# Adding DMAs and one tile at a time at the ends of an encoder's steps

## The chip, the core and the metric

The kernel runs on one core of a Trainium2 chip. The metric is the device time of one execution in microseconds. The core has five engines with an instruction stream each: TensorE (PE in the profile; its weight loads are PEld), VectorE (DVE), ScalarE (ACT), GpSimd (POOL) and SyncE (SP). Each engine works through its own stream in order, and streams wait for each other only through semaphores. DMAs are issued here from SyncE's stream, and those that add to what stands in the target from GpSimd's.

## What is computed

The reference is a trunk of two layers over 512 tokens of width 1024, in float32:

```
layer 0:  x += 0.5*ffn(norm(x));  x += mixer_s5_gla(norm(x));     x += 0.5*ffn(norm(x))
layer 1:  x += 0.5*ffn(norm(x));  x += mixer_retention(norm(x));  x += 0.5*ffn(norm(x))
out = norm(x)

norm(x) = x * rsqrt(mean(x*x) + 1e-6) * g
ffn(h)  = (silu(gate) * up) @ w2,   gate, up = split(h @ w1)      # hidden width 2816
```

The first mixer is a diagonal state space model (S5) beside a gated linear attention (GLA), with one projection in and one out. The second is a retention with eight heads. Each is run in both directions.

## The kernel before

All of x stays on the chip as eight tiles x[0] to x[7] of 128x512 (128 of the 1024 channels, by 512 tokens). Float32 products are made on TensorE as three products of rounded parts: mm3 (L196 to L198) multiplies high by high, high by low and low by high. So every operand is needed as a high and a low part. A weight unit (128x1024, 512 KB) is loaded by SyncE into `raw` (4 buffers), ScalarE casts it to `wh`, and `wl` = raw - wh is made in one of two ways (`weights`): by a subtraction on VectorE (L185, called plain), or by ScalarE writing -raw cast to `wl` (L191) and GpSimd issuing a DMA that adds raw to it (L192). Both `wh` and `wl` have 3 buffers.

The program has six steps, and this text calls their ends A to F: the first ffn (end A), the S5 and GLA mixer (end B), two ffns in a row by a scheme with seven products in place of eight blocks (`ffn7`; ends C and D), the retention mixer (end E), and a third ffn7 that finishes the output (end F). A step's last part makes the tiles of x one after the other. As soon as x[n] is there, `prep(n, ...)` makes the operands of the next step: `operand` one high and one low tile (L105, L106), and `operand7` the blocks that ffn7 needs. For tiles 0 to 3 these are b and n (L118 to L123). For tiles 4 to 7 they are ta, b2h, b2l, n23h, n23l and n4 (L130 to L139). Then `squares` (L158, L159) squares x[n] on ScalarE into a tile `sq` and adds it on GpSimd to `sumsq`.

The tiles sq, the difference of halves in `operand7` and its n4 all come from the pool with the tag `tb`, which has two buffers. The norm's factor is not applied to the operands. The next step begins with matmuls on the operands as they are, and somewhat later in TensorE's order stands a matmul of ones with `sumsq` (L166, `rstd`), from which the factor of each token comes. That matmul needs all eight squares. The instructions of each engine are put in order ahead of time, so the matmul's place is fixed.

The outputs of the mixers are matmuls with weight units of two tiles each (12 matmuls a tile and part). The first mixer's output has two parts, part 0 from GLA and part 1 from S5, which are summed in one bank of PSUM. The retention's output has four groups g of heads; each group's products are added to x by VectorE on their own (L1191).

Of the kernel before, what the change touches and what calls it, by code (L numbers as in the profile page):

```python
# [20 lines left out]
ALU = mybir.AluOpType  # L21
# [15 lines left out]
CHUNKS = ((0, 6), (6, 14), (14, 22))  # L37
# [13 lines left out]
def encoder(tc, I, out, dbg=None):  # L51
# [5 lines left out]
    with ExitStack() as ctx:  # L57
# [9 lines left out]
        x = [xs[:, i] for i in range(KT)]  # L67
# [30 lines left out]
        def bank(name="mm"):  # L98
            return pp.tile([128, S], F32, name=name, tag="mm")
# [50 lines left out]
                operand(i, n)  # L150
            squares(i, acc)

        def squares(i, acc):
            if i == 0:
                A.activation(acc, x[i], AF.Square)
            else:
                sq = tmp("tb")
                A.activation(sq, x[i], AF.Square)  # L158
                G.tensor_tensor(acc, acc, sq, op=ALU.add)  # L159

        def new_acc():
            return tp.tile([128, S], F32, name="sumsq", tag="sumsq", bufs=1)
# [114 lines left out]
        def ffn7(w1, w2, acc, nxt, pools, finish=None):  # L277
# [147 lines left out]
            for q, (ks0, ks1) in enumerate(CHUNKS):  # L425
                w2q = w2[0] if q == 0 else w2[1][q - 1]
                for j in range(ks0, ks1):
                    first, last = j == ks0, j == ks1 - 1
                    if j == 0:

                        three, rest = range(3), range(3, 4)
                        p1(0)
                        p1(1)
                        p2(0, three)
                        r2(0, three)
                    elif j != 1:
                        p1(j)
                    ready_22(j)
                    if j + 2 < ks1:
                        load(j + 2)  # L440
                    if not first:
                        r1(j - 1)
                        r3(j - 1)
                    if not last and j > 0:
                        ready_a1(j + 1)
                    ready_13(j)
                    if j == 0:
                        p2(0, rest)
                        r2(0, rest)
                    else:  # L450
                        p2(j)
                        if not last:
                            sums12(j + 1)
                        r2(j)
                        if j == 1:
                            rs = rstd(acc)
                    if not last:
                        if j == 0:
                            sums12(j + 1)
                        ready_2(j + 1)  # L460
                        sums34(j + 1)
                    else:
                        ws = [weights(w2q[n], True) for n in range(2)]
                    if not first:
                        r4(j - 1)
                    if not last:
                        ready_4(j + 1)
                    if not first:
                        a22(j - 1)
# [23 lines left out]
                    residual(n, pss[n], every)  # L493
                    done(n)
                for n in range(2, KT if more or finish is None else KT - 2):
                    w = weights(w2q[n], True)
                    ps = bank()
                    second(n, ps, w, range(ks0, ks1), ks1)
                    residual(n, ps, every)
# [249 lines left out]
        def s5_gla(acc, nxt, mp):  # L749
# [264 lines left out]

            banks = {}

            def project_out(part, n2, acc=None):
                h, l = weights(I["ab_out"][part, n2])
                for n in (n2 * 2, n2 * 2 + 1):
                    if part == 0:  # L1020
                        banks[n] = bank()
                    for k in range(4):
# [54 lines left out]
            project_out(1, 0, acc)  # L1077
            project_out(0, 2)
            project_out(1, 2, acc)
            project_out(0, 3)  # L1080
            project_out(1, 1, acc)
            project_out(1, 3, acc)
            return acc


        def retention(acc, nxt, mp):
# [109 lines left out]
            for g in range(4):  # L1196
# [13 lines left out]
                if 0 < g < 3:  # L1210
                    project_out(g - 1, outs.pop(g - 1), None)
                outs[g] += attend(2 * g + 1)
            project_out(2, outs.pop(2), None)
            acc = new_acc()
            project_out(3, outs.pop(3), acc)
            return acc

        def show(name):
# [24 lines left out]
        first = [unit[1:] for unit in first]  # L1243
        acc = new_acc()
        for i in range(KT):
            squares(i, acc)
        with tc.tile_pool(name="g0a", bufs=14) as ga:
            wk_pool = tc.tile_pool(name="s5work", bufs=1)
            wk = wk_pool.__enter__()
# [182 lines left out]
```

## Time and profile before

| | |
|---|---|
| time, median of 3 runs | 2152.77 us (2150.92 to 2152.77) |
| the profiled execution's own time | 2150.53 us |
| its span | 2148.7 us |
| its mean granted clock of TensorE | 0.988 |
| TensorE busy | 2085.6 us, 97% |
| VectorE busy | 1438.2 us, 67% |
| ScalarE busy | 1094.9 us, 51% |
| GpSimd busy | 265.9 us, 12% |

The span is the time between the first and the last instruction of the profiled execution, and its own time lies 1.8 us above it. Engines work side by side, so the shares don't add up. TensorE's idle time is short and stands in few places, and a share over the whole span doesn't show where.

### The profile page before, as it was taken

What the parts mean: (1) busy time and instruction counts of PE and PEld (TensorE: products, weight loads), DVE (VectorE), ACT (ScalarE), POOL (GpSimd) and SP (SyncE); (2) the same over time, 40 slices, a digit from 0 to 9 for tenths busy, and PEclk for the clock granted to TensorE, in tenths of its full rate; (3) what the DMA queues carried; (4) which work ended last, traced back from release to release, by engine and by line L of the source; (5) the groups of instructions that cost most, each with busy time, mean ns of one, the idle gap of its engine ahead of it and who ended that gap; (6) DMA issues with size and microseconds to landing.
All of it is one profiled execution on the core that took longest, in us unless ns stands there. A gap on an engine that the chain in (4) does not pass through costs nothing.

```text
span 2148.7 us, 31033 instructions
## 1 busy us (share of the span) xinstructions
PE 2085.6 (97%) x12088; PEld 1817.0 (85%) x12088; DVE 1438.2 (67%) x2256; ACT 1094.9 (51%) x1647; POOL 265.9 (12%) x281
## 2 busy tenths in 40 slices
PE   8999999988999999999999999999999998999998
PEld 6777888867888999997989899878888878899997
DVE  7697233457939968588868677555455559868584
ACT  7555332354377555455646364454444457555453
POOL 3442001101012000001000000100000012000001
PEclk9999999998999999999999999999999999999999
DMA  8988532458465464542545353534545454464541
GB/s 242 222 223 234 165 118 91 151 136 236 140 157 139 131 163 129 146 148 79 155 131 164 111 149 107 164 115 137 136 136 136 130 126 124 139 158 129 143 143 49
DMA packets 110083, 313.22 MB, mean 146 GB/s; under 512 B 18512, under 2 KB 33232, under 8 KB 109808
## 3 DMA queue, kind: packets, MB, share of 16 engines
q1 hardware_dynamic: 85168, 224.46, 30.8%
q0 software_dynamic: 24768, 86.78, 21.1%
q8 instruction: 95, 1.56, 0.3%
q14 instruction: 52, 0.43, 0.1%
HBM read 208.18 MB, written 14.14 MB: 103 GB/s over the span
## 4 chain that ended last, share of the span: by engine, by line
PE 77%; DVE 11%; DMA 4%; issue 4%; ACT 3%; POOL 1%; SPq 0%; DVEq 0%; ACTq 0%; POOLq 0%
PE mm L196 25%; PE mm L198 25%; PE mm L197 25%; DMA raw<-in_ffn_w_dram 2%; DMA wl<-raw 2%; DVE wl L185 0%; POOL sumsq L159 0%; ACT r13h L223 0%; DVE s L325 0%; DVE u L634 0%; ACT wl L191 0%; DVE n23l L137 0%; PE st L1167 0%; DVE s L319 0%; DVE s L324 0%
## 5 line engine op out<-in xcount | busy, mean ns | idle before, releaser
L183 ACT CAST wh<-raw 128x1024 fp32r<-128x1024 f32 (+1 forms) x227 | 232.2, 1027 | 402.2 <-PE mm L197 244.1
L196 PE MATMUL mm<-y,wh 128*128 128x512 f32 x776 | 309.8, 399 | 7.5 <-ACT wh L1239 5.0
L198 PE MATMUL mm<-y,wl 128*128 128x512 f32 x776 | 305.6, 394 | 5.6 <-DMA wl<-raw 5.6
L192 POOL DMA_DIRECT2D wl<-raw x159 | 137.6, 869 | 1401.2 <-ACT wl L191 987.3
L197 PE MATMUL mm<-y,wh 128*128 128x512 f32 x776 | 308.1, 397 | 0.1
L196 PE MATMUL mm<-g,wh 128*128 128x512 f32 (+1 forms) x672 | 258.6, 385 | 0.8 <-ACT g L223 0.8
L198 PE MATMUL mm<-g,wl 128*128 128x512 f32 (+1 forms) x672 | 258.5, 385 | 0.0
L197 PE MATMUL mm<-g,wh 128*128 128x512 f32 (+1 forms) x672 | 258.4, 384 | 0.0
L185 DVE TENSOR_TENSOR wl<-raw,wh 128x1024 fp32r<-128x1024 f32 (+1 forms) x131 | 154.1, 1178 | 119.7 <-ACT wh L183 115.4
L196 PEld LDWEIGHTS mm<-y,wh 128*128 128x128 f32 x776 | 147.0, 190 | 45.4 <-ACT wh L1239 5.5
L198 PEld LDWEIGHTS mm<-y,wl 128*128 128x128 f32 x776 | 146.9, 189 | 40.9 <-DMA wl<-raw 7.5
L191 ACT ACTIVATE wl<-raw 128x1024 fp32r<-128x1024 f32 x159 | 167.6, 1054 | 19.1 <-PE mm L197 19.1
L197 PEld LDWEIGHTS mm<-y,wh 128*128 128x128 f32 x776 | 147.2, 190 | 33.8 <-DVE y L106 1.9
L198 PEld LDWEIGHTS mm<-g,wl 128*128 128x128 f32 x672 | 126.2, 188 | 25.5
L197 PEld LDWEIGHTS mm<-g,wh 128*128 128x128 f32 x672 | 126.3, 188 | 25.3 <-DVE g L224 1.1
L196 PEld LDWEIGHTS mm<-g,wh 128*128 128x128 f32 x672 | 126.2, 188 | 25.2 <-ACT g L223 1.2
L405 DVE SCALAR_TENSOR_TENSOR ta<-mm,rs 128x512 f32<-128x512 f32 (+1 forms) x74 | 49.9, 675 | 99.3 <-PE mm L198 99.2
L159 POOL TENSOR_TENSOR sumsq<-sumsq,tb 128x512 f32<-128x512 f32 x47 | 72.1, 1535 | 341.0 <-ACT tb L158 333.5
L308 ACT CAST wh<-raw 128x1024 fp32r<-128x1024 f32 x63 | 66.1, 1050 | 59.5 <-PE mm L197 49.0
L353 ACT COPY sv<-mm 128x256 f32<-128x256 f32 x198 | 72.3, 366 | 47.3 <-PE mm L198 45.3
L224 DVE TENSOR_TENSOR r13l<-s,r13h 128x1024 fp32r<-128x1024 f32 x66 | 80.7, 1222 | 10.8 <-ACT r13h L223 10.7
L396 ACT ACTIVATE tb<-ta 128x512 f32<-128x512 f32 x66 | 41.7, 632 | 85.4 <-DVE ta L395 85.2
(393 smaller groups left out, 5542.9 us busy)
## 6 DMA issues: line engine op xcount, KB each, us to landing
raw<-in_ffn_w_dram SPq DMA_DIRECT2D x196, 512.0 KB, 3.3
wl<-raw POOLq DMA_DIRECT2D x159, 512.0 KB, 4.8
raw<-in_w2b_dram SPq DMA_DIRECT2D x48, 512.0 KB, 3.3
raw<-in_ret_in_dram SPq DMA_DIRECT2D x48, 512.0 KB, 3.3
raw<-in_w2a_dram SPq DMA_DIRECT2D x24, 384.0 KB, 3.4
raw<-in_ret_out_dram SPq DMA_DIRECT2D x16, 512.0 KB, 3.2
raw<-in_ab_in_dram SPq DMA_DIRECT2D x13, 512.0 KB, 3.4
wd<-wt SPq DMA_DIRECT2D x16, 256.0 KB, 5.2
```

The source lines that it names most:

```text
L159: G.tensor_tensor(acc, acc, sq, op=ALU.add)
L183: A.copy(h[:, c], raw[:, c])
L185: V.tensor_tensor(l[:, c], raw[:, c], f32(h[:, c]), op=ALU.subtract)
L191: A.activation(l, raw, AF.Copy, scale=-1.0)
L192: G.dma_start(l, raw, accum_op=ALU.add)
L196: T.matmul(ps, lh, rh, start=first, stop=False, skip_group_check=go_on)
L197: T.matmul(ps, lh, rl, start=False, stop=False, skip_group_check=go_on)
L198: T.matmul(ps, ll, rh, start=False, stop=last, skip_group_check=go_on)
L224: V.tensor_tensor(lo, src, f32(hi), op=ALU.subtract)
L308: A.copy(h, up)
L353: A.copy(z, ps[:, left])
L405: V.scalar_tensor_tensor(m[:, c], ps[:, c], 0.5, rs[:, c], op0=ALU.mult, op1=ALU.mult)
```

## The change

Three things are changed. `squares` issues a DMA from GpSimd's stream that adds the tile of squares to `sumsq`, where GpSimd added it itself; only the squares of the input, ahead of the first step, stay as they were. In the last part of each ffn7, the weight units of w2 get their low part by ScalarE and an adding DMA, where VectorE subtracted. And the last output tiles of both mixers are made in another order. In the first mixer both parts of tile 6, then both of tile 7, stand last. In the retention, groups 2 and 3 are summed in one bank of PSUM and added to x at once; tiles 0, 1, 4 and 5 get group 2 and later group 3, then tiles 2, 3, 6 and 7 get both groups one tile after the other.

```diff
--- before.py
+++ after.py
@@ -150,13 +150,16 @@
                 operand(i, n)
             squares(i, acc)
 
-        def squares(i, acc):
+        def squares(i, acc, first=False):
             if i == 0:
                 A.activation(acc, x[i], AF.Square)
             else:
                 sq = tmp("tb")
                 A.activation(sq, x[i], AF.Square)
-                G.tensor_tensor(acc, acc, sq, op=ALU.add)
+                if first:
+                    G.tensor_tensor(acc, acc, sq, op=ALU.add)
+                else:
+                    G.dma_start(acc, sq, accum_op=ALU.add)
 
         def new_acc():
             return tp.tile([128, S], F32, name="sumsq", tag="sumsq", bufs=1)
@@ -460,7 +463,7 @@
                         ready_2(j + 1)
                         sums34(j + 1)
                     else:
-                        ws = [weights(w2q[n], True) for n in range(2)]
+                        ws = [weights(w2q[n], q + 1 < len(CHUNKS)) for n in range(2)]
                     if not first:
                         r4(j - 1)
                     if not last:
@@ -493,7 +496,7 @@
                     residual(n, pss[n], every)
                     done(n)
                 for n in range(2, KT if more or finish is None else KT - 2):
-                    w = weights(w2q[n], True)
+                    w = weights(w2q[n], more)
                     ps = bank()
                     second(n, ps, w, range(ks0, ks1), ks1)
                     residual(n, ps, every)
@@ -1014,9 +1017,9 @@
 
             banks = {}
 
-            def project_out(part, n2, acc=None):
-                h, l = weights(I["ab_out"][part, n2])
-                for n in (n2 * 2, n2 * 2 + 1):
+            def project_out(part, n2, acc=None, w=None, tiles=(0, 1)):
+                h, l = w or weights(I["ab_out"][part, n2])
+                for n in (n2 * 2 + i for i in tiles):
                     if part == 0:
                         banks[n] = bank()
                     for k in range(4):
@@ -1077,9 +1080,11 @@
             project_out(1, 0, acc)
             project_out(0, 2)
             project_out(1, 2, acc)
-            project_out(0, 3)
             project_out(1, 1, acc)
-            project_out(1, 3, acc)
+            ws = [weights(I["ab_out"][part, 3]) for part in range(2)]
+            for i in range(2):
+                for part in range(2):
+                    project_out(part, 3, acc, ws[part], (i,))
             return acc
 
 
@@ -1210,9 +1215,31 @@
                 if 0 < g < 3:
                     project_out(g - 1, outs.pop(g - 1), None)
                 outs[g] += attend(2 * g + 1)
-            project_out(2, outs.pop(2), None)
+
             acc = new_acc()
-            project_out(3, outs.pop(3), acc)
+            banks = {}
+
+            def part(g, n, w):
+                h, l = w
+                if g == 2:
+                    banks[n] = bank()
+                for k4 in range(4):
+                    c = slice(((n % 2) * 4 + k4) * 128, ((n % 2) * 4 + k4 + 1) * 128)
+                    mm3(banks[n], h[:, c], l[:, c], *outs[g][k4], g == 2 and k4 == 0, g == 3 and k4 == 3)
+                if g == 3:
+                    V.tensor_tensor(x[n], x[n], banks[n], op=ALU.add)
+                    prep(n, nxt, acc)
+
+            for g in (2, 3):
+                for n2 in (0, 2):
+                    w = weights(I["ret_out"][g, n2])
+                    part(g, 2 * n2, w)
+                    part(g, 2 * n2 + 1, w)
+            for n2 in (1, 3):
+                ws = [weights(I["ret_out"][g, n2]) for g in (2, 3)]
+                for n in (2 * n2, 2 * n2 + 1):
+                    part(2, n, ws[0])
+                    part(3, n, ws[1])
             return acc
 
         def show(name):
@@ -1243,7 +1270,7 @@
         first = [unit[1:] for unit in first]
         acc = new_acc()
         for i in range(KT):
-            squares(i, acc)
+            squares(i, acc, True)
         with tc.tile_pool(name="g0a", bufs=14) as ga:
             wk_pool = tc.tile_pool(name="s5work", bufs=1)
             wk = wk_pool.__enter__()
```

What follows are pieces of the order of instructions on an engine, as the two programs have it; the changed program's line numbers are 3 higher in the first two pieces, and the addition of the retention's tiles stands at L1230 in the third. The first piece is GpSimd's stream at end C, before:

```order
L192 DMA wl<-raw 128x1024 x19
L159 TENSOR_TENSOR sumsq<-sumsq,tb 128x512 x3
L192 DMA wl<-raw 128x1024
L159 TENSOR_TENSOR sumsq<-sumsq,tb 128x512 x3
L192 DMA wl<-raw 128x1024
L159 TENSOR_TENSOR sumsq<-sumsq,tb 128x512
L192 DMA wl<-raw 128x1024 x19
```
and with the change:

```order
L195 DMA wl<-raw 128x1024 x23
L162 DMA sumsq<-tb 128x512
L195 DMA wl<-raw 128x1024 x2
L162 DMA sumsq<-tb 128x512
L195 DMA wl<-raw 128x1024
L162 DMA sumsq<-tb 128x512
L195 DMA wl<-raw 128x1024
L162 DMA sumsq<-tb 128x512
L195 DMA wl<-raw 128x1024
L162 DMA sumsq<-tb 128x512 x2
L195 DMA wl<-raw 128x1024
L162 DMA sumsq<-tb 128x512
```
Seven additions to sumsq (x2 and x3 are that many in a row) stood in two bunches between weights' DMAs, and now stand as DMAs among more of these. Each DMA that adds to sumsq waits until the one before it has landed.

The second piece is ScalarE's stream at the same end, with the semaphores that an instruction waits for (Pool is GpSimd, DMASW a DMA issued by GpSimd). Before:

```order
L158 ACTIVATE tb<-x 128x512 [waits Pool_49]
L138 CAST n_9171<-tb 128x256 [waits DVE_49]
L130 ACTIVATE ta<-x,columns 128x512 [waits DVE_49,Activation_49]
L223 CAST r2h<-s_9399 128x512 [waits DVE_49]
L132 CAST b2h<-ta 128x512 [waits Activation_49]
L308 CAST wh<-raw 128x1024 [waits DMAHW5_49,PE_49]
L130 ACTIVATE ta<-x,columns 128x512 [waits DVE_49]
L135 CAST n23h<-tc 128x512 [waits DVE_49]
L158 ACTIVATE tb<-x 128x512
L353 COPY sv<-mm 128x256 [waits PE_49]
L138 CAST n_9226<-tb 128x256 [waits DVE_49]
```
and with the change:

```order
L138 CAST n_9177<-tb 128x256 [waits DVE_49]
L311 CAST wh<-raw 128x1024 [waits DMAHW5_49,PE_49]
L130 ACTIVATE ta<-x,columns 128x512 [waits DVE_49,Activation_49]
L194 ACTIVATE wl<-raw 128x1024 [waits DMASW2_49,PE_49]
L132 CAST b2h<-ta 128x512 [waits Activation_49]
L130 ACTIVATE ta<-x,columns 128x512 [waits DVE_49]
L135 CAST n23h<-tc 128x512 [waits DVE_49]
L158 ACTIVATE tb<-x 128x512 [waits DMASW5_49]
L138 CAST n_9233<-tb 128x256 [waits DVE_49]
L132 CAST b2h<-ta 128x512 [waits Activation_49]
L356 COPY sv<-mm 128x256 [waits PE_49] x2
L135 CAST n23h<-tc 128x512 [waits DVE_49]
```
L158 is the square of a tile, of tiles 5 and 6 in the first fence and of tile 6 in the second. Tile 6's waited for nothing of its own before. With the change it waits for the landing of a DMA, which reads the buffer that it is to write, and the operands b2h and n23h (L132, L135) of tile 7 stand behind it.

The third piece is VectorE's stream at end E, up to the addition of the last tile of x. Before:

```order
L119 SCALAR_TENSOR_TENSOR b_16369<-x,columns,b_16369 128x256
L318 TENSOR_TENSOR s_16481<-raw 128x512
L324 TENSOR_TENSOR s_16481<-raw 128x512
L319 TENSOR_TENSOR s_16482<-s_16481,raw 128x512
L123 SCALAR_TENSOR_TENSOR n_16370<-tb,columns,n_16370 128x256
L325 TENSOR_TENSOR s_16483<-s_16482,raw 128x512
L224 TENSOR_TENSOR r2l<-s_16482,r2h 128x512
L131 SCALAR_TENSOR_TENSOR tc<-x,columns,ta 128x256
L134 TENSOR_TENSOR b2l<-ta,b2h 128x512
L224 TENSOR_TENSOR r4l<-s_16483,r4h 128x512
L133 SCALAR_TENSOR_TENSOR tc<-x,columns,tc 128x256
L1191 TENSOR_TENSOR x<-x,mm 128x512
```
and with the change:

```order
L1230 TENSOR_TENSOR x<-x,mm 128x512
L131 SCALAR_TENSOR_TENSOR tc<-x,columns,ta 128x256
L133 SCALAR_TENSOR_TENSOR tc<-x,columns,tc 128x256
L134 TENSOR_TENSOR b2l<-ta,b2h 128x512
L136 TENSOR_TENSOR tb<-ta,tc 128x256
L137 TENSOR_TENSOR n23l<-tc,n23h 128x512
L227 TENSOR_TENSOR wl<-raw,wh 128x1024
L139 TENSOR_TENSOR n_16396<-tb,n_16396 128x256
L321 TENSOR_TENSOR s_16481<-raw 128x512
L327 TENSOR_TENSOR s_16481<-raw 128x512
L322 TENSOR_TENSOR s_16482<-s_16481,raw 128x512
L1230 TENSOR_TENSOR x<-x,mm 128x512
```
The last rows x<-x,mm are tile 7's. The work on the next step's first weights (s, r2l, r4l, L318 to L325) stood ahead of it in part; now three of these rows do, and the tile before has its operands (b2l, n23l) done earlier.

## Rows read from the trace of the kernel before

**Rows 1.** The page, part 1: busy time, share of the span and instructions of each engine.

```profile
PE 2085.6 (97%) x12088; PEld 1817.0 (85%) x12088; DVE 1438.2 (67%) x2256; ACT 1094.9 (51%) x1647; POOL 265.9 (12%) x281
```

**Rows 2.** Stretches at five ends: window, its length, busy time (instructions) by engine, clock, DMA.

```profile
416.00:421.53 5.53, 5.53 (x25) 4.51 (x24) 3.18 (x4) 2.30 (x3) 1.53 (x1) 1.00 0.59 166
663.30:678.71 15.41, 11.53 (x75) 10.51 (x73) 14.58 (x26) 11.31 (x20) 3.90 (x3) 0.89 0.27 83
1009.20:1027.92 18.72, 13.96 (x98) 12.97 (x97) 17.23 (x28) 11.88 (x22) 5.28 (x4) 0.91 0.37 101
1356.48:1361.99 5.51, 5.51 (x25) 4.51 (x24) 2.14 (x3) 3.14 (x5) 2.16 (x2) 1.00 0.86 259
1784.97:1803.05 18.08, 12.53 (x76) 10.74 (x74) 17.85 (x29) 12.74 (x24) 7.52 (x5) 0.91 0.31 87
```

**Rows 3.** Who waited for whom, TensorE, 1005 to 1032 us: total, times, longest.

```profile
PE mm L196 <- ACT b2h L132: 2.7, 1, 2.7
PE mm L197 <- DVE b2l L134: 1.0, 1, 1.0
```

**Rows 4.** Who waited for whom, TensorE, 1780 to 1810 us.

```profile
PE mm L198 <- DVE r2l L224: 1.4, 1, 1.4
PE mm L196 <- ACT wh L308: 1.0, 1, 1.0
```

**Rows 5.** Ten 128x256 matmuls in a row, first and last: start, us, instruction.

```profile
1025.33 0.28 PE L197 MATMUL mm<-n,r13h 128*128 128x256 f32 x1
...
1026.39 0.28 PE L197 MATMUL mm<-n,r13h 128*128 128x256 f32 x1
```

**Rows 6.** The adds of squares, one line: durations in ns, first and last start.

```profile
L159 POOL TENSOR_TENSOR sumsq<-sumsq,tb x47: 1279/1517/2672, 10.8 to 2126.2; 128x512 f32<-128x512 f32 x47
```

**Rows 7.** Two lines of VectorE: a difference of tiles, and weights' low parts.

```profile
L137 DVE TENSOR_TENSOR n23l<-tc,n23h x12: 677/685/1787, 647.8 to 1800.7; 128x512 fp32r<-128x512 f32 x12
L185 DVE TENSOR_TENSOR wl<-raw,wh x131: 948/1222/1550, 200.8 to 2119.8; 128x1024 fp32r<-128x1024 f32 x107, 128x768 fp32r<-128x768 f32 x24
```

**Rows 8.** Adds of the retention mixer's output tiles, one line.

```profile
L1191 DVE TENSOR_TENSOR x<-x,mm x32: 629/687/689, 1524.8 to 1794.3; 128x512 f32<-128x512 f32 x32
```

**Rows 9.** Adding DMAs of 256 KB into y tiles (6, 36 to 88 us).

```profile
DMA to landing us min/median/max: 3.7/4.2/6.3
```

**Rows 10.** Adding DMAs of 256 KB into g tiles (7, 102 to 206 us).

```profile
DMA to landing us min/median/max: 3.9/4.9/7.1
```

**Rows 11.** Adding DMAs of 512 KB into wl, after 213 us: issue, and time to landing.

```profile
L192 POOL DMA_DIRECT2D wl<-raw x132: 852/859/880, 214.4 to 2064.5; - x132
DMA to landing us min/median/max: 4.4/4.6/12.3
```

**Rows 12.** GpSimd and TensorE at the end of the first step.

```profile
419.06 1.53 POOL L159 TENSOR_TENSOR sumsq<-sumsq,tb 128x512 f32<-128x512 f32 x1 [13.09 <-ACT tb L158]
421.30 0.39 PE L198 MATMUL mm<-y,wl 128*128 128x512 f32 x1
421.53 1.02 PE L166 MATMUL st<-sumsq,ones 128*128 128x512 f32 x2
```

**Rows 13.** GpSimd and TensorE at the end of the second seven-product step.

```profile
1359.75 1.29 POOL L159 TENSOR_TENSOR sumsq<-sumsq,tb 128x512 f32<-128x512 f32 x1
1361.99 1.02 PE L166 MATMUL st<-sumsq,ones 128*128 128x512 f32 x2
```

**Rows 14.** GpSimd and TensorE at the end of the last step.

```profile
2126.23 1.29 POOL L159 TENSOR_TENSOR sumsq<-sumsq,tb 128x512 f32<-128x512 f32 x1 [4.03 <-ACT tb L158]
2128.46 0.73 POOL L526 TENSOR_TENSOR sumsq<-sumsq,tb 128x256 f32<-128x256 f32 x1 [0.94 <-ACT tb L525]
2130.93 0.28 PE L1297 MATMUL st<-ones,sumsq 128*128 128x1 f32 x2
```

**Rows 15.** One weight of the retention mixer's output: ScalarE's cast, GpSimd's DMA.

```profile
1757.74 1.06 ACT L183 CAST wh<-raw 128x1024 fp32r<-128x1024 f32 x1 [2.81 <-PE mm L197]
1760.05 0.86 POOL L192 DMA_DIRECT2D wl<-raw  x1 [3.96 <-ACT wl L191]
```

## The prediction

> **What bounds the kernel now.** I began with the page's first part. TensorE is busy 97% of the span, VectorE 67%, ScalarE 51% and GpSimd 12% [rows 1], so time can only come from the few places where TensorE stands still. Neither program has more matmuls than the other, and only how they wait can differ. The edits touch the ends of steps, so I read next the stretch at each end, from the last matmul of the step's last tile to the rstd matmul [rows 2]. There a length beside TensorE's busy time and count shows whether it waited. At ends A and D, 5.5 us hold 25 matmuls of 128x512 without a gap. At B, C and E it waits, and VectorE is busy 14.58 of 15.41 us, 17.23 of 18.72 and 17.85 of 18.08. Then I read who is waited for. At C these are b2h and b2l of tiles 6 and 7 [rows 3], at E the weights r2l and wh [rows 4], and not the sum of squares. Ten matmuls of 128x256 in a row start 0.118 us apart [rows 5]. So 75, 98 and 76 of them need 8.9, 11.6 and 9.0 us, and the stalls are 6.6 us at B, 7.2 at C and 9.1 at E. End F is read below.
>
> The page doesn't name the cause that the change attacks. GpSimd's add of squares takes 1.28 to 2.67 us [rows 6]. While one runs, one VectorE operation with both inputs on the chip is stretched: n23l takes 685 ns in the median and 1787 at most [rows 7]. Seven adds at an end can cost VectorE some 7 x 1.1 = 7.7 us just where it is late.
>
> **The change part by part.**
>
> *VectorE is relieved.* Besides those 7.7 us, the eight low parts of w2 at the end of a seven-product step go to ScalarE and a DMA, at 1.22 us each [rows 7], 9.8 us. Five of them lie where C's lag builds up. At E eight additions of 0.69 us [rows 8] go. This is worth something at B, C and E alone, since TensorE doesn't wait for VectorE at A and D.
>
> *The chain of DMAs is new.* Each of the seven DMAs waits for the landing of the one before, and the last landing holds the rstd matmul. No DMA in the trace adds to sumsq. The nearest are 13 adding DMAs of the same size near the start: 3.7 us at least, 4.2 in the median and 6.3 at most into y [rows 9], and 3.9, 4.9 and 7.1 into g [rows 10]. Adding DMAs of twice the size take 4.4 us at least and 4.6 in the median later on [rows 11], so a lone one is near its minimum then. I take 3.9 us for a lone one (3.7 and that 0.2), and 4.4 where weights' DMAs are queued around it, just under the mean of the two medians. The bounds are 3.7 and 7.1. A handover (semaphore and start) costs some 0.1 us.
>
> A rule of the Trainium skill gives another price: its page "DMA: Bandwidth & Descriptors", section "Anatomy of one DMA — SWDGE (gpsimd) path", has 2.0 us plus the bytes over 436 GB/s, which is 2.6 us here by estimate. The rows never show less than 3.7. By 2.6 us there would be no new wait at A, D and F, and at best B's and C's stalls would go whole and E's to the 3.0 us below, for a time near 2130.
>
> *End A.* GpSimd starts on the last square at 419.06 and the rstd matmul starts at 421.53, one matmul (0.23 us) after the row before it [rows 12]; in the new order it stands one matmul later, at 421.76. With the DMA the sum is there at 419.06 + 3.9 + 0.1 = 423.06. **+1.3 us** (1.1 to 4.5).
>
> *End D.* GpSimd starts at 1359.75, rstd at 1361.99 [rows 13], four matmuls later in the new order: 1362.9. The DMA ends at 1363.75. **+0.9 us** (0.7 to 4.1).
>
> *End F.* The fifth tile's square is added at 2126.23, and GpSimd's add of the left half of the sixth starts at 2128.46, while the matmul that needs it starts at 2130.93 [rows 14]. Now that add waits for the landing at 2130.2 and ends 0.73 us later, at 2131.0. With the handover: **+0.2 us** (0 to 3.4).
>
> *End B.* In the new order, counted from the last matmul E, tile 4 ends at -19.1 us, tile 5 at -16.4, tiles 2 and 3 at -13.6 and -10.9, and 6 and 7 at -5.4 and 0. Two buffers of tb serve the squares and the operands' differences, so a square often waits until a DMA lands, and a hop is the DMA (4.4), the next square (0.6) and handovers (0.3), 5.3 us. Tile 4's square can start some 3 us behind its tile, at -16; six hops and two waits in ScalarE's order (1 us each by estimate) bring the last landing to +17.8. The rstd matmul stands 12 matmuls later than before, after 87 x 0.118 = 10.3 us of work. The stall is 7.5 us against 6.6: **+1.0 us** (-3.2 to +17). This takes the relief as given, and the chain as last.
>
> *End C.* Relieved, VectorE no longer lags when tile 4 comes. But in ScalarE's new order the square of tile 4 stands behind a cast into a weight buffer that tile 5's matmuls free at 998.2 us. I get that square at 1005, its landing at 1009.7, and then one hop each for tiles 5, 6 and 7, with ScalarE's order in between: 1014.3, 1019.5 to 1020.2, 1025.1. In the order tile 7's b2h stands behind tile 6's square, which waits for tile 5's landing. The rstd matmul ran at 1027.92 [rows 2]. **-2.8 us** (-5.6 with hops of 3.7, +8 with 7.1).
>
> *End E.* Tiles 6 and 7 now take both groups, and the weight unit of group 3 waits for a buffer that comes free only two parts, 5.4 us, before it is needed. One such unit went from its cast at 1757.74 to its DMA at 1760.05 [rows 15], 2.3 us, and the landing adds 4.4 (the least of [rows 11]) to 7.1 (the most of [rows 10]), 6.7 to 9.4 in all. That is a new stall of 1.3 to 4.0 us inside tile 6; I take 3.0, since other units' DMAs stand ahead in the queue. In return tile 6 and 7 lie 5.4 us apart where they were 2.7, VectorE is relieved, and the rstd matmul stands 12 matmuls later; the chain lands some 2 us after its 10.4 us of work. Stalls of 5.1 us against 9.1: **-4.0 us** (-7 to +5).
>
> What the low parts by DMA add is ScalarE 1.05 us each, beside matmuls, and a landing 10.9 us after the buffer is freed would still be in time, against 6.7 to 9.4. I take 0, and up to 2 us if one is late.
>
> **The sum.** 1.3 + 0.9 + 0.2 + 1.0 - 2.8 - 4.0 = -3.4 us. Of the profiled execution's 2150.5 us that leaves 2147.1, of the median 2152.8 it leaves 2149.4. I forecast 2148, in the middle. A measurement of this kernel can tell about 0.2%, 4.3 us, from no change, so this is about "the same", at its faster edge.
>
> **The rivals.**
>
> *1. Short hops: faster.* A DMA of 3.7 us throughout, so that the chain keeps pace with the tiles. For it speaks that most 512 KB ones are near their minimum after 213 us [rows 11]; against it, that weights' DMAs share the queue at B, C and E. A 1.1, D 0.7, F 0, B -3.2, C -5.6, E -6.8: -13.8, for 2137.
>
> *2. The chain holds up ScalarE: slower.* This is one mechanism, a hop that is longer than assumed, paid once at A, D and F and about four times at B, C and E, so some 15 times. The sum turns positive when a hop takes 0.23 us more than assumed, and passes +4.3 us at 0.5 more. For it speak the g tiles' median of 4.9 us [rows 10] and the in-order waits on tb; against it, [rows 11]. At 0.9 more it is -3.4 + 13.5 = +10, for 2160.
>
> The page "SBUF — State Buffer" of the Trainium skill, section "SBUF: two separate sides", would make hops longer: VectorE at work can keep GpSimd from writing a DMA's descriptors. Against it, the 132 issues in [rows 11] took 852 to 880 ns with VectorE busy two thirds of the time. It would be this rival, with its time.
>
> *3. The relief changes nothing.* TensorE waits at C for b2h, which ScalarE makes, and at E for wh. If ScalarE's order keeps these as late as they are, C and E give 1 us each, the rest stays, and the sum is +1.4: 2150.
>
> **How the numbers follow.** The forecast has 0.38, rival 1 0.28, rival 2 0.22, rival 3 0.12. Within the forecast's own spread (2142 to 2154) some 0.16 is more than 4.3 us faster. Faster: 0.28 + 0.16 = 0.44. Slower: nearly all of rival 2, 0.2. The same: 0.36. The forecast and rival 3 hold half the chance, and the range has to reach to where rivals 1 and 2 lie: 2137 to 2159 leaves out what lies beyond them, about 2 in 10.
>
> **What would show it.** Right: DMAs of 3.7 to 4.5 us into sumsq; n23l never above 0.8 us; waits of 1 to 2 us for the sum of squares ahead of rstd at A and D; at C and E fewer waits for b2l and r2l, and the sum of squares as the last releaser; a wait of about 3 us for wl in the retention's tile 6. Wrong: if squares wait long for tb on ScalarE, and b2h of tile 7 comes later than before, it is rival 2. If the squares are all there before rstd is, it is rival 1.

## The result, and the profile after

The changed kernel takes 2180.9 us in the median (2178.3 to 2181.6), beside 2151.9 us for the kernel before on the same chip: a ratio of 1.0138 with a 95% interval of 1.0123 to 1.0152. It is 29 us slower, where 3.4 us faster was forecast and 2159 us was the upper end of the range.

The profiled execution has a span of 2179.7 us against 2148.7, and the rstd matmuls show where the 31 us went. This table has their starts in the two traces (the first matmul on the sum in the last step for F).

| end | before, us | after, us | later by | added in the step |
|---|---|---|---|---|
| A | 421.53 | 427.23 | 5.7 | 5.7 |
| B | 678.71 | 689.99 | 11.3 | 5.6 |
| C | 1027.92 | 1051.68 | 23.8 | 12.5 |
| D | 1361.99 | 1394.45 | 32.5 | 8.7 |
| E | 1803.05 | 1833.46 | 30.4 | -2.1 |
| F | 2130.93 | 2162.60 | 31.7 | 1.3 |

In the new order the matmul stands later: one matmul of 0.23 us at A, 12 of 0.118 us at B and E (1.4 us), four of 0.23 us at D (0.9 us). The step up to it is longer by that and the next one shorter. For like work the six steps are +5.5, +4.4, +13.9, +7.8, -2.5 and +2.7 us. A to D make the loss.

The first lines of the page after, and two of its DMA issues (size, median us from issue to landing), answer to [rows 1] and [rows 11].

```profile
PE 2096.2 (96%) x12088; PEld 1822.8 (84%) x12088; DVE 1393.6 (64%) x2226; ACT 1114.7 (51%) x1669; POOL 258.4 (12%) x303
...
wl<-raw POOLq DMA_DIRECT2D x181, 512.0 KB, 5.0
...
sumsq<-tb POOLq DMA_DIRECT2D x40, 256.0 KB, 3.9
```

VectorE has 45 us less to do than before and ScalarE 20 us more, and there are 22 more weights' DMAs (159 before) and 40 into sumsq. Nothing of that is near a bound as a share.

Who waited for whom on TensorE, at A, C, D and around E (total us, times, longest), answers to [rows 3, 4].

```profile
PE st L169 <- DMA sumsq<-tb: 4.8, 1, 4.8
...
PE mm L199 <- ACT b2h L132: 4.1, 1, 4.1
PE mm L201 <- DMA wl<-raw: 3.9, 2, 2.7
PE st L169 <- DMA sumsq<-tb: 0.6, 1, 0.6
...
PE st L169 <- DMA sumsq<-tb: 6.3, 1, 6.3
...
PE mm L201 <- DMA wl<-raw: 2.7, 1, 2.7
```

At A and D TensorE now waits 4.8 and 6.3 us for the last square, where it waited for nothing. At C it waits 4.1 us for b2h, 2.7 before, and 3.9 us for weights' low parts, none before. The wait for wl of 2.7 us inside the retention's tile 6 is there as forecast. The sum is not what TensorE waits for at B and E, and at C for 0.6 us alone.

GpSimd and TensorE at end A, in order of time, answer to [rows 12].

```profile
419.66 0.86 POOL L162 DMA_DIRECT2D sumsq<-tb  x1 [13.53 <-ACT tb L158]
...
427.23 2.07 PE L169 MATMUL st<-sumsq,ones 128*128 128x512 f32 x2 [4.85 <-DMA sumsq<-tb]
...
429.53 0.63 PE L201 MATMUL mm<-y,wl 128*128 128x512 f32 x1
429.95 0.63 PE L199 MATMUL mm<-y,wh 128*128 128x512 f32 x1
```

The DMA is issued at 419.66 and the matmul starts when it has landed, at 427.23. The adding DMA took 7.5 us, not 3.9.

The next rows are stretches of the changed kernel, each from the issue of one adding DMA into sumsq to its landing: its length, then the engines' busy time, and at the end the granted clock, the mean busy share of the DMA engines and what they moved in GB/s.

```profile
389.53:392.73 3.20, 3.20 (x15) 2.60 (x14) 1.23 (x1) 0.65 (x1) 0.86 (x1) 1.00 0.49 92
405.27:408.47 3.20, 3.20 (x15) 2.60 (x15) 1.23 (x1) 1.05 (x1) 0.86 (x1) 1.00 0.46 85
419.66:427.19 7.53, 2.72 (x12) 1.88 (x11) 1.45 (x2) 2.33 (x2) 1.47 (x2) 0.85 0.78 213
1035.67:1038.88 3.21, 0.00 (x0) 0.00 (x0) 3.21 (x8) 3.10 (x5) 0.86 (x1) 1.00 0.46 86
1027.98:1035.13 7.15, 7.15 (x44) 6.28 (x42) 3.31 (x6) 2.63 (x5) 0.86 (x1) 0.93 0.93 298
1364.32:1371.18 6.86, 6.86 (x32) 5.68 (x31) 2.44 (x4) 3.68 (x5) 1.72 (x2) 1.00 1.08 254
1383.14:1390.64 7.50, 5.01 (x22) 3.76 (x20) 2.01 (x3) 3.86 (x5) 1.75 (x2) 1.00 1.02 268
1391.16:1394.40 3.24, 0.00 (x0) 0.00 (x0) 0.00 (x0) 0.00 (x0) 0.86 (x1) 0.50 0.60 110
2141.17:2150.46 9.29, 9.29 (x42) 7.70 (x41) 3.20 (x4) 3.76 (x5) 1.21 (x2) 1.00 0.81 167
```

In these rows a landing takes 3.2 us where the DMA engines are half idle and move 80 to 110 GB/s, and 6.9 to 7.5 us where they move 213 GB/s and more. By the same measure, the 16 of the 40 with less than 140 GB/s took 3.2 to 3.9 us, and the 13 with more than 200 took 3.9 to 7.8. So the traffic goes with the time, but doesn't set it alone. The longest, 9.3 us, lies between, at 167 GB/s, issued half a microsecond behind a weights' DMA. Over all 40 the times are these:

```profile
L162 POOL DMA_DIRECT2D sumsq<-tb x40: 859/862/1212, 329.3 to 2158.4; - x40
...
DMA to landing us min/median/max: 3.2/3.9/9.3
```

The relief of VectorE is there. Its operation n23l is never stretched now, where the longest took 1787 ns [rows 7]:

```profile
L137 DVE TENSOR_TENSOR n23l<-tc,n23h x12: 678/684/686, 655.3 to 1828.2; 128x512 fp32r<-128x512 f32 x12
```

But at C VectorE waits for a landing, since the sum tb of tile 5 needs a buffer that a DMA still reads:

```profile
DVE tb L136 <- DMA sumsq<-tb: 4.0, 1, 4.0
```

The addition of tile 6 to x stands behind that, and b2h of tile 6 behind the addition.

There is an earlier and longer wait at C. VectorE stands still for 7.7 us, up to 1014.65, for the load of a weight unit of the next step, and in its order the additions of tiles 4 and 5 to x, and so their squares, stand behind it:

```profile
DVE s L321 <- DMA raw<-in_ffn_w_dram: 7.7, 1, 7.7
```

In the kernel before no such wait stands there. It belongs to the second edit, as the experiments show.

At D the whole chain is late. The last two squares are done on ScalarE at 1379.0 and 1384.7, and their DMAs are issued 4.1 and 6.5 us later, each half a microsecond behind the landing of the one before:

```profile
1384.05 0.61 ACT L158 ACTIVATE tb<-x 128x512 f32<-128x512 f32 x1
...
1383.14 0.86 POOL L162 DMA_DIRECT2D sumsq<-tb  x1 [5.55 <-DMA sumsq<-tb]
1391.16 0.86 POOL L162 DMA_DIRECT2D sumsq<-tb  x1 [6.28 <-issue]
```

The last DMA takes only 3.2 us (1391.16 to 1394.40 above). TensorE waits at D because the five hops before it were long, 4.5 to 7.8 us.

### The profile page after: what moved, and what is told of

Its sections match the earlier page's. It is cut to its first block, busy times and chain, and to the rows that moved or that the text cites. A ratio compares the mean times of both kernels' runs of the same rounds, so it can differ in the third digit from the quotient of the medians.

```text
span 2179.7 us, 31084 instructions
## 1 busy us (share of the span) xinstructions
PE 2096.2 (96%) x12088; PEld 1822.8 (84%) x12088; DVE 1393.6 (64%) x2226; ACT 1114.7 (51%) x1669; POOL 258.4 (12%) x303
## 4 chain that ended last, share of the span: by engine, by line
PE 48%; DVE 7%; DMA 7%; ACT 3%; issue 3%; POOL 0%; DVEq 0%; POOLq 0%; ACTq 0%; SPq 0%
PE mm L199 16%; PE mm L200 16%; PE mm L201 16%; DMA sumsq<-tb 3%; DMA raw<-in_ffn_w_dram 3%; DMA raw<-in_w2b_dram 1%; DVE s L328 1%; DVE s L322 1%; DVE s L327 1%; ACT r13h L226 1%; DVE s L321 1%; DMA wl<-raw 1%; ACT g L226 0%; ACT wl L194 0%; DVE r13l L227 0%
## 5 line engine op out<-in xcount | busy, mean ns | idle before, releaser
L195 POOL DMA_DIRECT2D wl<-raw x181 | 156.8, 870 | 1520.8 <-ACT wl L194 1097.2
L188 DVE TENSOR_TENSOR wl<-raw,wh 128x1024 fp32r<-128x1024 f32 (+1 forms) x109 | 126.5, 1162 | 121.4 <-ACT wh L186 120.3
L194 ACT ACTIVATE wl<-raw 128x1024 fp32r<-128x1024 f32 x181 | 190.8, 1054 | 19.2 <-PE mm L200 19.2
L227 DVE TENSOR_TENSOR r13l<-s,r13h 128x1024 fp32r<-128x1024 f32 x66 | 80.6, 1221 | 13.1 <-ACT r13h L226 12.9
L226 ACT CAST r2h<-s 128x512 fp32r<-128x512 f32 x66 | 41.0, 621 | 77.6 <-DVE s L322 77.6
```

What stands on the lines that cost most here:

```text
L188: V.tensor_tensor(l[:, c], raw[:, c], f32(h[:, c]), op=ALU.subtract)
L194: A.activation(l, raw, AF.Copy, scale=-1.0)
L195: G.dma_start(l, raw, accum_op=ALU.add)
L226: A.copy(hi, src)
L227: V.tensor_tensor(lo, src, f32(hi), op=ALU.subtract)
```

## The experiments

All times are medians, and ratios, with their 95% intervals, are to the kernel before, run beside each on the same chip (2149.1 to 2150.3 us). The code cuts are excerpts: they show the changed lines and leave the rest out.

**Undoing and doing the edits.** The first four runs take the change apart.

*squares_gpsimd*: the first edit undone.

```diff
-                G.dma_start(acc, sq, accum_op=ALU.add)
+                G.tensor_tensor(acc, acc, sq, op=ALU.add)
```

> The change with its first edit undone: GpSimd adds the squares itself again; the low parts by DMA and the new order stay. Theory 1 (the DMAs that add squares are what costs: each lands 3.2 us after its issue when alone, but 7 to 9 us beside other transfers, and rstd waits for the last): the waits for the sum at ends A and D (5.0 and 6.5 us in the change) go, C loses most of its 12 us, and the time is within 6 us of the kernel before, 2150 to 2158 us. Theory 2 (the low parts by DMA cost as much: they make wl late and fill the queue): 2160 us or more, with waits for wl of 3 to 4 us left at C and no gain there. Rival 3 (the new order costs): 2160 us or more with the loss at B and E.

Measured: 2164.2 us, 1.0072 (1.0057 to 1.0087). So the first edit is about half of the loss. What is left is more than theory 1 allows, and theory 2's time holds beside it, though the waits for wl at C are 2.1 us. The waits for the sum at A and D are gone.

*lows_vector*: the second edit undone.

```diff
-                    w = weights(w2q[n], more)
+                    w = weights(w2q[n], True)
```

> The change with its second edit undone: VectorE subtracts the low parts of w2 in the last part of a seven-product step again; squares by DMA and the new order stay. Theory 1: A keeps its wait of 5 us, since no weight's DMA is near it; at D the squares' DMAs land sooner with the eight weights' DMAs gone, and the wait of 6.5 us shrinks to 1 to 3 us; the time is 2163 to 2172 us. Theory 2: C and D come back to the kernel before, and only A's 5 us are left, 2153 to 2158 us. Rival 3: no change, 2180 us.

Measured: 2166.6 us, 1.0082 (1.0067 to 1.0097), as theory 1 has it. A keeps 4.9 us of waiting; D has 3.6 us, a little over the 1 to 3 expected.

*order_only*: the third edit alone.

> The third edit alone on the kernel before: the new order of the mixers' last tiles. Theories 1 and 2: B and E gain as forecast or a little less, 2144 to 2151 us, with a new wait for wl of about 3 us in the retention's tile 6. Rival 3: the order itself costs, 2155 us or more, with the loss at B.

Measured: 2151.1 us, 1.0007 (0.9998 to 1.0017). The order neither gains nor costs much; the gain of 2 to 5 us did not come.

*squares_only*: the first edit alone.

> The first edit alone on the kernel before: squares added by DMA. Theory 1: A waits 5 us, B and E wait longer for the sum than in the change, since the last tiles lie 2.7 us apart there and the seven DMAs are one behind the other; 2165 to 2178 us. Theory 2: A's 5 us and little else, 2153 to 2158 us. In both, n23l on VectorE is never stretched above 0.8 us.

Measured: 2173.8 us, 1.0117 (1.0100 to 1.0133), theory 1. TensorE's waits in it at A, C and D:

```profile
PE st L169 <- DMA sumsq<-tb: 5.2, 1, 5.2
...
PE st L169 <- DMA sumsq<-tb: 3.1, 1, 3.1
PE mm L199 <- ACT b2h L132: 1.7, 1, 1.7
...
PE st L169 <- DMA sumsq<-tb: 4.4, 1, 4.4
```

The sum is waited for at each of these ends, and b2h at C less than before (1.7 against 2.7). With the new order the first edit costs 15.6 us (lows_vector against order_only), alone 24.7. The second edit costs 13.1 us (squares_gpsimd against order_only).

**Why a landing is long.** *copies_beside* adds traffic where there was little. Squares are added by DMA, and at end A:

```diff
                     G.dma_start(acc, sq, accum_op=ALU.add)
+                    if phase[0] == 0 and len(beside) < 6:
+                        beside.append(i)
+                        for cp in range(3):
+                            dma(spare[cp], sq)
```

> Squares by DMA alone, and at end A three plain copies of each of the first six tiles of squares to a scratch in memory are issued by SyncE at the moment at which GpSimd issues the adding DMA. Theory 1 (an adding DMA is long beside other transfers): the hops of these six tiles, which took 3.2 us with nothing beside them, take 5 to 8 us; they lie 14 us apart, so the time stays that of squares by DMA alone, 2174 us. Rival (the long landings belong to the queue of GpSimd, its order or its semaphores): the hops stay at 3.2 us, since no other DMA of GpSimd is near.

The six DMAs ahead of the last at A without the copies (squares_only), issue and landing:

```profile
L162 POOL DMA_DIRECT2D sumsq<-tb x6: 859/859/859, 329.8 to 405.8; - x6
...
DMA to landing us min/median/max: 3.2/3.2/5.0
```

and with them:

```profile
L162 POOL DMA_DIRECT2D sumsq<-tb x6: 859/859/862, 327.7 to 403.7; - x6
...
DMA to landing us min/median/max: 3.5/4.6/6.4
```

Each of the six lands later than its like without copies, by 0.3 to 2.0 us, and the median goes from 3.2 to 4.6 us. So transfers of another queue do make an adding DMA land later, and the rival falls. It is less than the 5 to 8 us that I expected, although the DMA engines moved 234 to 272 GB/s in these six stretches, more than the 213 at A in the change. So what makes 7.5 us there, beyond traffic as such, was not shown. One run of the whole took 2175.0 us.

**Which of the landings cost.** *squares_split* has DMAs for tiles 1 to 4 and GpSimd's own adds for 5 to 7; *squares_not7* has GpSimd add only the last tile's.

```diff
-                if first:
+                if first or i > 4:      # squares_split; i > 6 in squares_not7
                     G.tensor_tensor(acc, acc, sq, op=ALU.add)
```

> Squares by DMA alone, but for tiles 1 to 4 only; GpSimd adds those of tiles 5 to 7 itself. Theory 1 (only the late landings ahead of rstd cost): no wait for the sum at A and D, C, B and E within 2 us of the kernel before, 2147 to 2155 us. Rival (the DMAs cost wherever they stand, by holding buffers of tb and so ScalarE's and VectorE's order): 2160 us or more, with b, n and b2h waited for at B, C and E.

> Squares by DMA alone, but GpSimd adds the last tile's itself. Theory 1a (the landing of the last DMA, ahead of rstd, is most of the first edit's loss of 24 us): A's wait is gone, D's and C's are cut by 3 to 5 us each, 2158 to 2163 us. Theory 1b (the whole chain is late, the last DMA no more than the others): A's wait goes and C, D and E keep theirs, 2166 us or more.

Measured: squares_split 2157.6 us, 1.0035 (1.0022 to 1.0048); squares_not7 2157.1 us, 1.0034 (1.0021 to 1.0047). Taking one DMA of seven away, the last, gives back 17 of the 24.7 us. Nothing waits at A and D in squares_not7, and at C:

```profile
PE mm L199 <- ACT b2h L132: 1.3, 1, 1.3
PE mm L200 <- DVE b2l L134: 1.0, 1, 1.0
```

That is less than before the change (2.7 for b2h), so VectorE's relief is worth 1.4 us in this wait. The 7 us that remain in both runs were not expected. In each run's one profiled execution half or more of what is lost arises in the middle of a step, far from any square. In squares_not7 an adding DMA for a weight's low part, issued at 762.0, takes 9.0 us where the like one before took 4.4 (issued at 761.7). TensorE waits 2.6 us for it, and its granted clock is 0.66 over the 5 us behind. In squares_split TensorE waits 2.1 us for VectorE's ta near 1178. Whether every execution has these stalls, one trace can't show.

**Why low parts by DMA cost.** *lows_only* is the second edit alone, *lows_first2* the same for the first two of the eight units.

> The second edit alone on the kernel before: low parts of w2 by DMA. From the runs so far it makes about 10 to 13 us, 2159 to 2163 us, most of it between rstd of the first and of the second seven-product step, with waits for wl at C and D and for ScalarE's copies sv. If it acts only together with the new order, 2150 us.

Measured: 2165.5 us, 1.0072 (1.0056 to 1.0089). TensorE's waits at C, and at D:

```profile
PE mm L196 <- ACT b2h L132: 3.7, 1, 3.7
PE mm L198 <- DMA wl<-raw: 2.6, 2, 1.9
...
PE mm L198 <- DMA wl<-raw: 1.0, 1, 1.0
```

The waits for wl are 2.6 and 1.0 us, and the wait for b2h is 1.0 us longer than before. A longer wait stands behind these: an adding DMA reads `raw` until it lands, and SyncE can't load the next unit into that buffer earlier. Waits of SyncE, VectorE and ScalarE from 975 to 1020 us:

```profile
SPq L294 <- DMA wl<-raw: 21.7, 5, 7.2
DVE s L318 <- DMA raw<-in_ffn_w_dram: 6.4, 1, 6.4
ACT qh L223 <- DMA raw<-in_ffn_w_dram: 6.8, 2, 6.4
```

In the kernel before SyncE waits there once for a landing (7.2 us), and VectorE and ScalarE not at all for a load. The first of these loads starts at 989.93 here and at 981.81 there, 8 us earlier. VectorE reaches tile 4's addition to x only behind this wait.

> The second edit for the first two of the eight units only, whose loads stand far ahead of their use. Theory 2d (wl lands late where a unit must follow the release of a buffer within two tiles): no loss, 2149 to 2153 us. Rival (any unit by DMA at this place costs, by the queue and ScalarE's order): 2153 us or more, a fourth of 15 us.

Measured: 2151.8 us, 1.0007 (0.9998 to 1.0017): no loss that can be told from none. The other six units carry it. VectorE waits for no load at C in this run.

*negate_extra* gives ScalarE its part of the work without the DMAs, on top of the new order.

```diff
                 A.copy(h[:, c], raw[:, c])
+                if extra:
+                    A.activation(l[:, c], raw[:, c], AF.Copy, scale=-1.0)
                 if plain:
                     V.tensor_tensor(l[:, c], raw[:, c], f32(h[:, c]), op=ALU.subtract)
```

> The new order alone, and ScalarE also writes the negated weights of the eight units, as it does ahead of an adding DMA, while VectorE still subtracts their low parts over it. So ScalarE's share of the second edit is there without its DMAs and without VectorE's relief. Theory 2a (the DMAs' landings make the second edit's loss of 13 us): like the new order alone, 2151 us, within 4. Theory 2b (ScalarE's extra 1.05 us a unit, ahead of copies and casts that TensorE waits for, makes it): 2158 us or more, with waits for sv and b2h on ScalarE at C and D.

Measured: 2154.2 us, 1.0019 (1.0009 to 1.0028), 2 to 3 us over the new order alone. Theory 2a holds for the most part; ScalarE's work makes about a fourth by the medians, with intervals that overlap. But the wait for b2h at C is 3.5 us here, without any of the DMAs, and 2.8 with the new order alone. So most of the longer wait for b2h in lows_only (3.7) can come from ScalarE's work.

*raw_held* keeps raw's buffer until a DMA has landed, while wl is made by VectorE.

```diff
                     V.tensor_tensor(l[:, c], raw[:, c], f32(h[:, c]), op=ALU.subtract)
+                    if held:
+                        G.dma_start(spare[:, c], raw[:, c])
```

> The kernel before, and each of the eight raw units of w2 at the end of a seven-product step is also copied by a DMA of GpSimd's to a scratch in memory, behind VectorE's subtraction. So wl is made by VectorE and in time, but raw's buffer stays held until a DMA has landed, GpSimd's queue has the eight DMAs, and the traffic is there. Theory 2c (the second edit costs by holding raw's four buffers, so that SyncE loads the next units later): 2158 us or more, with waits for raw's loads on ScalarE. Theory 2d (it costs because wl itself lands late): 2150 to 2154 us.

Measured: 2150.6 us, 1.0004 (0.9995 to 1.0012). Eight more DMAs in GpSimd's queue cost nothing that shows. Theory 2c is not settled by this run, because the loads that matter weren't held back. Waits of SyncE and ScalarE from 975 to 1020 us:

```profile
SPq L298 <- DMA wl<-raw: 7.3, 1, 7.3
ACT qh L227 <- DMA raw<-in_ffn_w_dram: 0.3, 1, 0.3
```

The first of the loads for the next step starts at 981.70, as in the kernel before (981.81), and SyncE waits for no copy in this stretch. The sign that theory 2c names, waits for raw's loads, is missing here and stands in lows_only.

**The order.** *order_ret* and *order_s5* are the two halves of the third edit. *order_plain4* is the whole order, with one low part in each seven-product step made by VectorE. *ret_plain4* is the retention's half with that low part. The cut is that of the last two.

```diff
-                        ready_a1(j + 1)
+                        ready_a1(j + 1, j == 3)
```

> The retention's half of the third edit alone on the kernel before. The forecast gave it -4.0 us. In the run of the new order alone the stretch up to rstd at E was 5.0 us shorter and the step behind it 4.9 us longer, of which 1.4 us each way are 12 matmuls that changed sides: so -1 to +1 us, 2148 to 2152.

> The S5 and GLA mixer's half of the third edit alone on the kernel before. The forecast gave it +1.0 us. In the run of the new order alone the step up to rstd at B was 1.0 us shorter and the step behind it 4.9 us longer: so +1 to +4 us, 2151 to 2154.

> The whole new order, and in each seven-product step the low part of the fifth unit of gate weights (index 4) is subtracted by VectorE, where an adding DMA that took 8.1 us left TensorE waiting 2.8 us for it behind E. If the gain at E is given back by that wait, this is 2 to 3 us faster than the new order alone, 2147 to 2149 us, and a little faster than the kernel before; if the wait only moves to the next late thing (g behind rstd), 2151 us.

> The two parts that helped together: the retention's half of the new order, and the low part of the fifth unit of gate weights by VectorE in each seven-product step. If they add, -2 and -4 us, 2144 to 2146 us; if both gain by the same wait, 2147 to 2149 us.

Measured: order_ret 2148.5 us, 0.9989 (0.9981 to 0.9998); order_s5 2153.0 us, 1.0012 (1.0004 to 1.0021); order_plain4 2147.0 us, 0.9988 (0.9980 to 0.9997); ret_plain4 2145.7 us, 0.9975 (0.9966 to 0.9984). The retention's half gains 1.8 us and the other loses 2.6. TensorE's waits for weights by DMA from 1770 to 1880 us, in order_ret:

```profile
PE mm L198 <- DMA wl<-raw: 4.6, 2, 2.5
```

and in ret_plain4:

```profile
PE mm L198 <- DMA wl<-raw: 2.1, 1, 2.1
```

One of the two waits, 2.5 us long, is gone. It took back about 1 us of the order's gain, since the same matmul waits in the kernel before as well (1800 to 1880 us):

```profile
PE mm L198 <- DMA wl<-raw: 1.6, 1, 1.6
```

ret_plain4 is 4.6 us faster than the kernel before, where the change is 29 us slower, and it is the fastest kernel of the study. Its time is what was expected if the two gains add; the low part alone, on the kernel before, was not run.

## Why the prediction was wrong, by its steps

**What bounds the kernel** was read rightly: the ends of steps are where the two kernels differ.

The stalls of 6.6, 7.2 and 9.1 us that I took from [rows 2] were too large as something to win: the waits in them are 3.8 us at B, 4.8 at C and at most 5.5 at E, and the rest is TensorE at work, in part at a lower clock (0.89 to 0.91 there).

**VectorE's relief** came as described, n23l at 686 ns at most and 45 us less work, but it was worth little: 1.4 us in the wait for b2h at C (squares_not7). Rival 3 had that part right. (Its time was added wrongly: its sum of +1.4 us gives 2153 by the base of the forecast, not 2150.)

**The price of a hop** is the first step that failed. I took 3.9 us for a lone DMA and 4.4 among weights' DMAs. The median is 3.9, by luck, since a lone one takes 3.2 and many take 5 to 9. At A I took the last DMA for a lone one, and in GpSimd's queue it is. The traffic there is SyncE's, the next mixer's tables and weights, which start when the step ends, and it landed after 7.5 us. [rows 2] had the traffic in the last two columns, 166 GB/s at A and 259 at D against 83 to 101 at B, C and E, and I read those rows for TensorE alone. copies_beside shows that another queue's transfers lengthen an adding DMA. At D I overlooked that a weights' DMA of GpSimd stands 1 us ahead of the last add, in the kernel before already:

```profile
1358.76 0.87 POOL L192 DMA_DIRECT2D wl<-raw  x1 [3.15 <-ACT wl L191]
```

**Ends A and D**, forecast at +1.3 and +0.9 us (to 4.5 and 4.1 at most), are waits of 4.8 and 6.3 us, and some 2 us each for the clock behind them (below). At A it is the last landing. At D a second step failed: I let the last DMA start when GpSimd's add had started, as if the chain kept pace with the tiles. In the change it doesn't, and the last DMA, itself short, starts 6.5 us behind its square. With the first edit alone (squares_only), which has fewer weights' DMAs there, the last DMA's own 6.8 us make the wait of 4.4.

**Ends B and C**, forecast at +1.0 and -2.8, came out at +4.4 and +13.9 us from rstd to rstd, for like work. At B the forecast had the chain last, and TensorE doesn't wait for it. At C two things of the forecast are there: the square of tile 4 is late, and a landing holds up an engine's order ahead of b2h. But the square is late because VectorE waited 7.7 us for a load, and the forecast had it wait for a cast. And the engine that the landing holds up, for 4.0 us, is VectorE, with the buffer of tb. On top came 3.9 us of waiting for wl.

**The low parts by DMA**, taken as 0 and 2 us at most, cost 13 to 15 us, and this is the third step that failed. I held a margin, 10.9 us from the buffer's release, against wl alone. That margin counts for a unit whose negation starts at once, and ScalarE comes to it in its own order; but waits for wl itself are only 3.6 of the 15 us in lows_only. What I left out is the other end of the DMA: it holds `raw`, the next step's first weights load 8 us later, and VectorE and ScalarE stand still for 6.4 us in front of them. The two units with the most lead cost nothing that shows, and cause no such wait. ScalarE's work is some 2 to 3 us. How much of the 13 to 15 us the late loads make was not isolated by a run: the trace shows the wait, and raw_held, which was meant to test it, didn't bring it about.

**End E**, forecast at -4.0, is -2.5 in the change for like work, but the retention's half alone gains 1.8 us over the whole kernel. The new stall for wl was forecast at 3.0 and is 2.7. With the new order alone, E's 3.5 us are given back whole in the step behind it (+3.4, table below); about 1 us of that is one low part that comes later, and the rest is open.

**End F**, +0.2, came out at +2.7 us over its whole step.

**Rival 2** was the mechanism of the first edit's half, with a chance of 0.22. It was sized wrongly, because it made all hops longer by the same amount, and no rival had the second edit's half. The rule of the Trainium skill that would have made hops longer (page "SBUF — State Buffer", section "SBUF: two separate sides") is not what happened: of 40 issues into sumsq 38 took 859 to 919 ns and two 1212, 862 in the median. The 2.6 us by the Trainium skill's page "DMA: Bandwidth & Descriptors", section "Anatomy of one DMA — SWDGE (gpsimd) path", lie below every landing here, though as near to the lone hop of 3.2 us as my 3.9.

**What adds up and what stays open.** On top of the new order the edits add: 2.0 + 15.6 + 13.1 = 30.7 us against 29.0. By steps, in one profiled execution each, the edits alone differ from the kernel before by these us, for like work (the rstd matmul's place counted as above; two executions can differ by 1 us and more in a step):

| | A | B | C | D | E | F |
|---|---|---|---|---|---|---|
| first edit (squares_only) | +6.4 | +3.7 | +5.4 | +7.0 | +5.2 | 0.0 |
| second edit (lows_only) | +0.4 | -0.7 | +4.9 | +7.2 | -0.2 | +2.8 |
| third edit (order_only) | -0.9 | +0.4 | +3.5 | -1.0 | -3.5 | +3.4 |
| the change | +5.5 | +4.4 | +13.9 | +7.8 | -2.5 | +2.7 |

At A, B and C the edits add up. At D the first two alone would make 14 us and make 7.8 together. That the first edit alone costs 9 us more than with the new order is spread over several steps: at E it is 5.2 us against 2.0 (lows_vector less order_only). That the chain has more time there with the new order is argued. What makes the order's 3.5 us at C stays open, too.

## What to carry to other kernels

A DMA in a serial chain ahead of an instruction that TensorE reaches in order must be priced at the traffic of that moment, of all queues. Here the ends of steps were when the next step's loads started, and the rate of the DMA engines in the very stretch before the change gave a warning, though not the time. Ask also whether the chain keeps pace: at D the last link was short and started late. Moving work from a busy engine to a DMA trades a cost in throughput for one in latency; the last link, one of seven, made two thirds of the first edit's loss alone. A DMA has two ends: a margin for its result counts from when the issuing engine gets to it in its own order, and the buffer that it reads is free only when it has landed, so ask which load waits for that buffer, and who stands in order behind the load.

## What the runs showed of the hardware

TensorE's granted clock fell while it waited for the landing and came back late. In the wait at D (1391.16 to 1394.40 in the rows above) it is 0.50, the lower of the two levels, 1.2 GHz, after TensorE had stood still since 1388. The stretches behind the waits at A (two) and D (two):

```profile
427.23:430.00 2.77, 2.77 (x5) 1.54 (x6) 0.00 (x0) 0.66 (x1) 0.00 (x0) 0.50 0.56 163
430.00:434.00 4.00, 4.00 (x16) 3.18 (x14) 3.91 (x2) 0.03 (x1) 0.62 (x1) 0.79 0.92 336
1394.45:1398.00 3.55, 3.55 (x7) 2.18 (x8) 0.72 (x1) 0.69 (x1) 0.00 (x0) 0.54 0.92 323
1398.00:1402.00 4.00, 4.00 (x19) 3.26 (x18) 3.93 (x3) 0.43 (x1) 0.00 (x0) 1.00 0.12 41
```

Matmuls of 128x512 start 0.42 us apart there (429.53 and 429.95 above), where 0.23 us is usual, so behind the wait at A some 4.5 us of TensorE's work pass at about half speed, and behind that at D some 3 us, which by estimate costs half of that. Of the five stretches of the kernel before, the lowest has 0.89 [rows 2].

An adding DMA of 256 KB inside the chip takes 3.2 us at least, from the start of an issue of 0.86 us, and up to 9.3 us. The 13 of that size in the kernel before took 3.7 us at least [rows 9].
